# An encoder layer on one core: large tiles on multiples of 512 bytes, and another way into the first and out of the last matmul

## The chip, the cores and the metric

One core of a Trainium2 chip runs the whole program. The metric is the device time of one execution in microseconds (us), the median of three runs. A core has five engines that work side by side: TensorE (PE, matmuls, with its weight loads shown apart as PEld), VectorE (DVE), ScalarE (ACT), GpSimd (POOL) and SyncE (SP, which here only issues DMAs). They read and write the on-chip memory (SBUF, 128 partitions), TensorE writes its results to eight PSUM banks of 128 x 512 floats.

## The reference

One encoder layer over 256 tokens of 2048 features, in float32: a SwiGLU feed-forward block (FFN) with half weight, a mixer (a Hyena convolution group beside a differential-attention group), and a second FFN, with a layer norm behind each.

```python
x = layer_norm(ALPHA * x + 0.5 * swiglu(x, ffn1_w_gate, ffn1_w_up, ffn1_w_down), ln1_g, ln1_b)
y = hybrid_mixer(x, w_in, ..., w_out, lam_init)
x = layer_norm(ALPHA * x + y, ln2_g, ln2_b)
x = layer_norm(ALPHA * x + 0.5 * swiglu(x, ffn2_w_gate, ffn2_w_up, ffn2_w_down), ln3_g, ln3_b)

def swiglu(x, w_gate, w_up, w_down):
    return (jax.nn.silu(x @ w_gate) * (x @ w_up)) @ w_down      # D_FF = 5632
def layer_norm(x, g, b):
    mu = jnp.mean(x, -1, keepdims=True); var = jnp.mean(jnp.square(x - mu), -1, keepdims=True)
    return (x - mu) * lax.rsqrt(var + 1e-5) * g + b
```

## The kernel before

**Arithmetic.** Every float32 operand of a matmul is split into a rounded high part (`hi`, made by ACT as a cast) and the rest (`lo`, made by DVE as a subtraction). A product is hi x hi + hi x lo + lo x hi: three matmuls (`mm3`), or two where the stream side holds `[hi | lo]` side by side (`xx[:, k]`, 512 columns), as in the gate and up projections (`ws_block`: L368 with 512 columns, L369 with 256).

**Weights.** All weights pass through a list of units of 512 KB. `fetch` issues the DMA of a unit on SP into one of four `raw` buffers, `prepare` issues its cast and subtraction (L171, L172), `nextunit` hands it to the matmuls. A unit of a gate or up matrix holds 4 k-tiles of 256 columns, one of a down matrix 2 k-tiles of 512 columns. `halves` cuts the DMA and the split of the first two units into two.

**Order.** The kernel is written in program order; small side jobs are put between units (`beside`, `tick`). Instructions of one engine then run in the order in which the scheduler of the language has laid them down; `after(a, b)` holds a behind b on its engine.

**Head.** The transposed input `x_t` comes in eight pieces of 2 k-tiles (256 KB, tiles `xt0`), all on SP, with the first weight units between them. `xt_chunk("0", c, ...)` casts and subtracts them into `xx`. Twelve matmuls on a tile of ones (`warm(12)`, each shown as two rows, L296) keep TensorE busy until then.

**Down projection and layer norm.** `as_chunk` makes the output in four chunks of 512 columns (c = 0 to 3), for two groups of tokens (j = 0, 1). For the last `lead` units of chunk 3 `as_block` does all of j = 0 before j = 1, so that the sums of j = 0 are read while TensorE still works on j = 1. `add_rows` adds a chunk to the residual `res` (L323) and takes its statistics (L324); `ln_stats` makes mean and 1/sigma (L328, L330, a power on POOL at L331). `last_rows` does this for chunk 3. Between layers `normalise` and `xt_chunk` follow: subtract the mean and scale, transpose on TensorE, apply g and b, split.

**Tail.** After the last FFN `finish(j, c, on_pool)` writes the result: for chunks 0 to 2 two DVE operations, (res - mean) x g (L1024) and x 1/sigma + b (L1025); for chunk 3 one ACT operation and two POOL operations (L1020 to L1022). Each chunk leaves by a DMA of 256 KB from SP (L1026).

**Memory.** SBUF is given out in the order of the pools: `const` (`res` 16 KB per partition, `xx` 32 KB, `ident`, `ones`, `mhalf` of 8 bytes, two `pvt`, `stats` of 192 bytes), then the weight buffers, then the small tiles, then the FFN's `hh` and `hl`. In the built program `res` and `xx` begin 128 bytes behind a multiple of 512, the weight and `xt0` buffers 352 bytes behind one (32 behind a multiple of 64), `hh` and `hl` 416 behind one.

Of the kernel before, what the change touches and what calls it, by code (L numbers as in the profile page):

```python
# [17 lines left out]
P = 128  # L18
# [56 lines left out]
def kernel(ctx: ExitStack, tc: tile.TileContext, a: dict, out: bass.AP):  # L75
# [69 lines left out]
    def halves(i, k):  # L145

        return [slice(0, k // 2), slice(k // 2, k)] if i < 2 else [slice(0, k)]

# [9 lines left out]
    def prepare(n):  # L158
        while st["split"] < min(n, len(units)):
            i = st["split"]  # L160
            _, k, c, name = units[i]
            late = i - (len(units) - LEAD)
            if 0 <= late < 4:

                hi, lo = (xx[:, 4 * late + 2 * q:4 * late + 2 * q + 2].rearrange("p k a l -> p k (a l)") for q in range(2))
            else:
                hi = wp.tile([P, k, c], F32R, tag="whi", name=f"hi{name}")
                lo = wp.tile([P, k, c], F32R, tag="wlo", name=f"lo{name}")
            raw = raws.pop(i)
            for s_ in halves(i, k):  # L170
                i1 = nc.scalar.copy(out=hi[:, s_], in_=raw[:, s_])  # L171
                i2 = nc.vector.tensor_tensor(out=lo[:, s_], in0=raw[:, s_], in1=hi[:, s_].bitcast(F32), op=ALU.subtract)  # L172
# [55 lines left out]
    nc.gpsimd.memset(ones, 1.0)
    mhalf = const.tile([P, 2], F32, name="mhalf")
    nc.gpsimd.memset(mhalf, -0.5)  # L230
# [31 lines left out]
    hy_g = [pvt[1][:, NV + i:NV + i + 1] for i in range(8)]  # L262

    def xt_chunk(tag, c, g, b):
        for kp in (2 * c, 2 * c + 1):
            hs = xx[:, 2 * kp:2 * kp + 2, 0, :]
            ls = xx[:, 2 * kp:2 * kp + 2, 1, :]
            if g is None:
                i1 = nc.scalar.copy(out=hs, in_=xt0[kp])
# [48 lines left out]

    stats = const.tile([P, 2, 4, 6], F32, name="stats")

    def add_rows(ps, j, c, scale):
        cs = slice(c * 512, (c + 1) * 512)
        nc.vector.scalar_tensor_tensor(out=res[:, j, cs], in0=ps, scalar=scale, in1=res[:, j, cs], op0=ALU.mult, op1=ALU.add)  # L323
        nc.vector.bn_stats(out=stats[:, j, c, :], in_=res[:, j, cs])  # L324

    def ln_stats(tag, j):
        mv = sm.tile([P, 2], F32, tag="mv", name=f"mv{tag}{j}")
        nc.vector.bn_aggr(out=mv, in_=stats[:, j, :, :])  # L328
        rs = sm.tile([P, 1], F32, tag="rs", name=f"rs{tag}{j}")
# [44 lines left out]

    def as_block(pd, lhs, use, n_k):

        for j in range(2):
            for k0, (h, lo) in use:
                for k in range(2):
                    kk = k0 + k  # L380
                    xh_, xl_ = lhs(kk, j)
                    mm3(pd[j], xh_, xl_, h[:, k, :], lo[:, k, :], kk == 0, kk == n_k - 1)

    def as_chunk(pd, lhs, n_k, lead=1):
# [4 lines left out]
        use = [(ku * 2, nextunit()) for ku in range(n - lead, n)]  # L389
        as_block(pd, lhs, use, n_k)  # L390


    def ffn(tag, first, down_side=None, gate_side=None, filler=None, lead=2):
        with tc.tile_pool(name=f"ffn{tag}", bufs=1, reuse_waits="tile") as fp:
# [616 lines left out]

    ln = ffn("3", first2, last_vectors(), lead=LEAD)
    ov = out[0].rearrange("(p j) d -> p j d", j=2)

    def finish(j, c, on_pool):
        cs = slice(c * 512, (c + 1) * 512)
        r, gt, bt = res[:, j, cs], gb3["ln3_g", c], gb3["ln3_b", c]
        mean, rs, nm = ln[j]
        if on_pool:
            nc.scalar.activation(out=r, in_=r, func=AF.Identity, bias=nm, scale=rs)  # L1020
            nc.gpsimd.tensor_tensor(out=r, in0=r, in1=gt, op=ALU.mult)  # L1021
            nc.gpsimd.tensor_tensor(out=r, in0=r, in1=bt, op=ALU.add)  # L1022
        else:
            nc.vector.scalar_tensor_tensor(out=r, in0=r, scalar=mean, in1=gt, op0=ALU.subtract, op1=ALU.mult)  # L1024
            nc.vector.scalar_tensor_tensor(out=r, in0=r, scalar=rs, in1=bt, op0=ALU.mult, op1=ALU.add)  # L1025
        nc.sync.dma_start(out=ov[:, j, cs], in_=r)  # L1026

    for j in range(2):
        nc.vector.scalar_tensor_tensor(out=ln[j][2], in0=ln[j][0], scalar=-1.0, in1=ln[j][1], op0=ALU.mult, op1=ALU.mult)
# [30 lines left out]
```

## Time and profile before

| what | value |
|---|---|
| median of 3 runs | 1960.94 us (1959.08 to 1961.29) |
| the profiled execution | 1963.29 us, of which 1961.2 us are the span that the profile shows |
| TensorE busy in the span | 1932.8 us (99%), 10,260 matmul rows |
| DVE, ACT, POOL busy | 62%, 47%, 16% |
| DMA | 376.43 MB, 192 GB/s on average, 57.6% of 16 DMA engines on SP's queue |
| first matmul on data / end of the last one | 8.05 us / 1946.95 us after the span's start |
| mean granted TensorE clock | 0.995 |

How to read it: times are counted from the span's start. A timeline row has start, duration, engine, line, operation, output<-inputs, shape, and in brackets how long the engine was idle before and what released it. Durations of matmuls overlap; the distance between two starts is what one costs. A row of windows has the stretch, its length, the busy time of PE, PEld, DVE, ACT and POOL with their instruction counts, the granted clock (1.00 is full speed), the DMA share and GB/s. The 1963.29 us of the profiled execution are the span and 2.1 us around it, and 2.35 us above the median.

### The profile page before, as it was taken

The numbers are of one execution on the slowest core, as the hardware profiler recorded it, in microseconds if no ns is written. First come the engines' busy times: TensorE is split into PE (matmuls) and PEld (weight loads), VectorE is DVE, ScalarE is ACT, GpSimd is POOL, SyncE is SP. The second block draws the span as 40 slices with busy tenths as digits, with TensorE's granted clock in tenths as the row PEclk, the third lists the DMA queues.
The fourth block names the chain that finished last, engine by engine and source line by source line (L and its number), as shares of the span: only waits on it lengthen the run. The fifth ranks groups of instructions, "written<-read, shape, count | busy, mean of one in ns | idle before, by whom it ended". The sixth has DMA issues, their size and how long they took to land. (4 is left out here: it accounts for less than half of the span.)

```text
span 1961.2 us, 27062 instructions
## 1 busy us (share of the span) xinstructions
PE 1932.8 (99%) x10260; PEld 1656.4 (84%) x10260; DVE 1215.4 (62%) x1538; ACT 926.1 (47%) x1334; POOL 305.3 (16%) x330
## 2 busy tenths in 40 slices
PE   9999999999999999999999999999999999999997
PEld 8888888888888887888887878888888888888885
DVE  5555556555566656899978666755555555544445
ACT  5554444544444435545555534545444544433332
POOL 4221111121100002012222011312111121100001
PEclk9999999999999999999999999999999999999999
DMA  8656656656666656655575444865656556555553
GB/s 288 204 187 192 190 189 198 192 185 193 203 208 214 204 191 207 220 181 153 172 226 161 158 154 157 274 191 187 192 191 193 187 189 194 187 189 187 189 186 115
DMA packets 294698, 376.43 MB, mean 192 GB/s; under 512 B 13263, under 2 KB 222312, under 8 KB 294568
## 3 DMA queue, kind: packets, MB, share of 16 engines
q1 hardware_dynamic: 289832, 361.90, 57.6%
q0 software_dynamic: 4736, 12.82, 2.2%
q8 instruction: 80, 1.31, 0.3%
q14 instruction: 50, 0.41, 0.1%
HBM read 366.27 MB, written 8.39 MB: 191 GB/s over the span
## 5 line engine op out<-in xcount | busy, mean ns | idle before, releaser
L368 PE MATMUL ps<-xx,hi1g 128*128 128x512 f32 x1408 | 490.2, 391 | 1.5 <-ACT hi1g L171 1.5
L368 PE MATMUL ps<-xx,hi2g 128*128 128x512 f32 x1408 | 488.6, 390 | 1.1 <-DVE xx L95 1.1
L369 PE MATMUL ps<-xx,lo1g 128*128 128x256 f32 x1408 | 397.4, 283 | 0.1
L369 PE MATMUL ps<-xx,lo2g 128*128 128x256 f32 x1408 | 397.0, 282 | 0.0
L172 DVE TENSOR_TENSOR lo2g<-raw2g,hi2g 128x1024 fp32r<-128x1024 f32 x176 | 234.8, 1335 | 179.6 <-ACT hi2g L171 179.6
L172 DVE TENSOR_TENSOR lo1g<-raw1g,hi1g 128x1024 fp32r<-128x1024 f32 (+1 forms) x178 | 232.5, 1308 | 177.6 <-ACT hi1g L171 177.6
L368 PEld LDWEIGHTS ps<-xx,hi1g 128*128 128x128 f32 x1408 | 264.8, 188 | 58.2 <-ACT hi1g L171 1.7
L368 PEld LDWEIGHTS ps<-xx,hi2g 128*128 128x128 f32 x1408 | 264.3, 188 | 56.4 <-ACT xt L282 1.3
L171 ACT CAST hi2g<-raw2g 128x1024 fp32r<-128x1024 f32 x176 | 185.0, 1052 | 187.3 <-PE ps L368 174.9
L171 ACT CAST hi1g<-raw1g 128x1024 fp32r<-128x1024 f32 (+1 forms) x178 | 185.2, 1042 | 179.7 <-PE ps L368 170.7
L369 PEld LDWEIGHTS ps<-xx,lo1g 128*128 128x128 f32 x1408 | 266.7, 190 | 0.7 <-DVE lo1g L172 0.5
L369 PEld LDWEIGHTS ps<-xx,lo2g 128*128 128x128 f32 x1408 | 266.1, 189 | 0.1
L404 POOL TENSOR_TENSOR hf<-hf,sg 128x256 f32<-128x256 f32 x88 | 64.7, 755 | 741.8 <-DVE hf L373 741.7
L172 DVE TENSOR_TENSOR lo2d<-raw2d,hi2d 128x1024 fp32r<-128x1024 f32 x84 | 103.6, 1233 | 118.7 <-ACT hi2d L171 118.7
L171 ACT CAST hi1d<-raw1d 128x1024 fp32r<-128x1024 f32 x88 | 92.4, 1050 | 132.0 <-PE pd L92 119.7
L171 ACT CAST hi2d<-raw2d 128x1024 fp32r<-128x1024 f32 x84 | 88.4, 1052 | 138.7 <-PE pd L92 131.0
L172 DVE TENSOR_TENSOR lo1d<-raw1d,hi1d 128x1024 fp32r<-128x1024 f32 x88 | 107.2, 1221 | 72.7 <-ACT hi1d L171 72.7
L90 PE MATMUL pd<-hi1d,hh 128*128 128x512 f32 x352 | 139.3, 396 | 0.0
L368 PE MATMUL ph<-xx,hihy 128*128 128x512 f32 x384 | 137.0, 397 | 2.2 <-DVE xx L95 1.1
L92 PE MATMUL pd<-hi1d,hl 128*128 128x512 f32 x352 | 139.1, 395 | 0.0
L91 PE MATMUL pd<-lo1d,hh 128*128 128x512 f32 x352 | 139.1, 395 | 0.0
L90 PE MATMUL pd<-hi2d,hh 128*128 128x512 f32 x336 | 132.9, 395 | 0.0
(380 smaller groups left out, 3078.8 us busy)
## 6 DMA issues: line engine op xcount, KB each, us to landing
raw1d<-in_ffn_w_down_dram SPq DMA_DIRECT2D x88, 512.0 KB, 4.3
raw2g<-in_ffn_w_gate_dram SPq DMA_DIRECT2D x88, 512.0 KB, 3.5
raw2g<-in_ffn_w_up_dram SPq DMA_DIRECT2D x88, 512.0 KB, 3.5
raw2d<-in_ffn_w_down_dram SPq DMA_DIRECT2D x88, 512.0 KB, 4.2
raw1g<-in_ffn_w_gate_dram SPq DMA_DIRECT2D x87, 512.0 KB, 3.5
raw1g<-in_ffn_w_up_dram SPq DMA_DIRECT2D x87, 512.0 KB, 3.9
rawhy<-in_w_in_dram SPq DMA_DIRECT2D x48, 512.0 KB, 4.5
rawat<-in_w_in_dram SPq DMA_DIRECT2D x48, 512.0 KB, 4.2
```

Of the source, the lines that this page charges most:

```text
L90: mm(out=o, lhsT=lh, rhs=rh, start=start, stop=False)
L91: mm(out=o, lhsT=lh, rhs=rl, start=False, stop=False)
L92: mm(out=o, lhsT=ll, rhs=rh, start=False, stop=stop)
L171: i1 = nc.scalar.copy(out=hi[:, s_], in_=raw[:, s_])
L172: i2 = nc.vector.tensor_tensor(out=lo[:, s_], in0=raw[:, s_], in1=hi[:, s_].bitcast(F32), op=ALU.subtract)
L368: mm(out=ps[t], lhsT=h[:, k, ts_], rhs=xx[:, kk].rearrange("p a l -> p (a l)"), start=kk == 0, stop=False)
L369: mm(out=ps[t][:, :L], lhsT=lo[:, k, ts_], rhs=xx[:, kk, 0, :], start=False, stop=kk == KD - 1)
L404: nc.gpsimd.tensor_tensor(out=hf, in0=hf, in1=sg, op=ALU.mult)
```

## The change

Four edits come together.

1. **Places in SBUF.** The small constants move ahead of `res` and `xx`, two unused spaces are put in (`line`), `nlam` and `g08` leave the mixer's pool, the filter's three weights share one `t512` buffer. In the built program `res`, `xx`, all weight buffers, the `t512` buffers, `hh`, `hl` and the mixer's large tiles then begin at a multiple of 512 bytes.
2. **Head.** The first two pieces of `x_t` are issued from ACT's queue, the first as two DMAs of one k-tile; unit 0 comes in four pieces; the second piece of x is cast behind the first two quarters of unit 0 (`xt_first`).
3. **Last chunk of the FFNs and of the output projection.** For j = 1 chunk 3 is two halves of 256 columns in two PSUM banks (`last_banks`). In the last `lead` units the first half is done whole before the second (`apart`).
4. **Tail.** ACT and POOL no longer take part in chunk 3. For j = 1 the multiplication with g of chunks 2 and 3 is done ahead of the statistics where it can be (`times_g`); b - mean/sigma x g for these 1024 columns is made by TensorE as a product of a 2 x 128 tile (rows: -mean/sigma, and ones) with a 2 x 256 tile (rows: g and b), four times (`pb`); DVE then does x 1/sigma + that, in pieces of 512, 256 and 256 columns.

```diff
+    def line(pool, n):
+        pool.tile([P, n // 4], F32, name="space", tag="space", bufs=1)
     def halves(i, k):
-        return [slice(0, k // 2), slice(k // 2, k)] if i < 2 else [slice(0, k)]
+        n = (4, 2)[i] if i < 2 else 1
+        return [slice(q * k // n, (q + 1) * k // n) for q in range(n)]
...
+                if i == 0 and s_.stop == 2:
+                    xt_first(1, i1, i2)
...
+    mhalf = const.tile([P, 2], F32, name="mhalf")
+    stats = const.tile([P, 2, 5, 6], F32, name="stats")
+    line(const, 384 - 32 - 256)
+    ident = const.tile([P, P], F32, name="ident")
...
-        nc.sync.dma_start(out=xt0[kp], in_=a["x_t"][:, 2 * kp:2 * kp + 2, :])
+        if kp == 0:
+            for i in range(2):
+                nc.scalar.dma_start(out=xt0[kp][:, i], in_=a["x_t"][:, i, :])
+        else:
+            (nc.scalar if kp == 1 else nc.sync).dma_start(out=xt0[kp], in_=a["x_t"][:, 2 * kp:2 * kp + 2, :])
...
+    def xt_first(kp, a1=None, a2=None):
+        hs = xx[:, 2 * kp:2 * kp + 2, 0, :]
+        ls = xx[:, 2 * kp:2 * kp + 2, 1, :]
+        for k_ in ([slice(0, 1), slice(1, 2)] if kp == 0 else [slice(0, 2)]):
+            i1 = nc.scalar.copy(out=hs[:, k_], in_=xt0[kp][:, k_])
+            i2 = sub(nc.vector, ls[:, k_], xt0[kp][:, k_], hs[:, k_])
...
-    def last_rows(tag, pd, scale):
+    def last_rows(tag, pd, scale, between=None):
         ln = []
-        for j in range(2):
-            add_rows(pd[j], j, 3, scale)
-            ln.append(ln_stats(tag, j))
+        add_rows(pd[0], 0, 3, scale)
+        ln.append(ln_stats(tag, 0))
+        for half in range(2):
+            add_rows(pd[1][half], 1, 3, scale, half)
+            if between is not None and half == 0:
+                between()
+        ln.append(ln_stats(tag, 1))
...
+        go(pd[0], 0, slice(0, 512), ks)
+        if not isinstance(pd[1], list):
+            go(pd[1], 1, slice(0, 512), ks)
+            return
+        for ks_ in ([ks] if apart else [[k] for k in ks]):
+            for half in range(2):
+                go(pd[1][half][:, :256], 1, slice(half * 256, (half + 1) * 256), ks_)
...
+    def ln_rows():
+        nc.gpsimd.memset(lh2, 1.0)
+        for q in range(4):
+            t = sm.tile([P, L], F32, tag="sg" if q < 2 else "hf", name=f"gb2_{q}")[:2]
+            for r, nme in enumerate(("ln3_g", "ln3_b")):
+                nc.gpsimd.dma_start(out=t[r:r + 1, :], in_=a[nme][0:1, 1024 + q * L:1024 + (q + 1) * L])
...
+    def early_g():
+        times_g(1, 2)
+        times_g(1, 3, 0)
...
-    for j in range(2):
-        nc.vector.scalar_tensor_tensor(out=ln[j][2], in0=ln[j][0], scalar=-1.0, in1=ln[j][1], op0=ALU.mult, op1=ALU.mult)
-        for c in range(4):
-            finish(j, c, c == 3)
+    for c in range(4):
+        centre(0, c)
+        scale_add(0, slice(c * 512, (c + 1) * 512), gb3["ln3_b", c])
+    mean, rs, nm = ln[1]
+    centre(1, 0)
+    after(times_g(1, 3, 1), last["rs"])
+    nc.vector.scalar_tensor_tensor(out=nm, in0=mean, scalar=-1.0, in1=rs, op0=ALU.mult, op1=ALU.mult)
+    pn = bank("pn")
+    mm(out=pn[:1, :P], lhsT=nm, rhs=ident, start=True, stop=True)
+    nc.scalar.copy(out=lh2[:1, :], in_=pn[:1, :P])
+    pb = [bank(f"pb3_{i}") for i in range(2)]
+    for q in range(4):
+        mm(out=pb[q // 2][:, q % 2 * L:(q % 2 + 1) * L], lhsT=lh2, rhs=gb2[q], start=True, stop=True)
+    scale_add(1, slice(0, 512), gb3["ln3_b", 0])
+    centre(1, 1)
+    scale_add(1, slice(512, 1024), gb3["ln3_b", 1])
+    scale_add(1, slice(1024, 1536), pb[0])
+    for q in range(2):
+        scale_add(1, slice(1536 + q * L, 1536 + (q + 1) * L), pb[1][:, q * L:(q + 1) * L])
```

How the order moves, at three places. ACT at the start of the program before (`xt_0`, `xt_1` are the pieces of x, `raw1g_0_0` is unit 0 and `raw1g_0_1` unit 1; the last column is partitions x elements):

```order
L269 ACT_TABLE_LOAD
L269 CAST xx<-xt_0_71 128x2x256
L269 CAST xx<-xt_1_76 128x2x256
L171 CAST hi1g_0_0_140<-raw1g_0_0_73 128x512 x2
L269 CAST xx<-xt_2_78 128x2x256
L171 CAST hi1g_0_1_146<-raw1g_0_1_80 128x512 x2
```

And ACT at the start now:

```order
L238 DMA xt_0_78<-in_x_t_dram 128x256 x2
L240 DMA xt_1_86<-in_x_t_dram 128x512
L285 ACT_TABLE_LOAD
L285 CAST xx<-xt_0_78 128x256 x2
L176 CAST hi1g_0_0_145<-raw1g_0_0_81 128x256 x2
L285 CAST xx<-xt_1_86 128x2x256
L176 CAST hi1g_0_0_145<-raw1g_0_0_81 128x256 x2
L176 CAST hi1g_0_1_157<-raw1g_0_1_90 128x512 x2
L285 CAST xx<-xt_2_88 128x2x256
```

Half of unit 0 no longer stands behind the second piece of x, and unit 1 no longer behind the third; three DMA issues stand ahead of the table load.

DVE behind the last matmul before (`pd_3_1` is chunk 3 of j = 1):

```order
L323 SCALAR_TENSOR_TENSOR res<-pd_3_1_16759,res 128x512
L324 BN_STATS stats<-res 128x6
L328 BN_AGGR mv_17144<-stats 128x2
L330 TENSOR_SCALAR rs_17146<-mv_17144 128x1
L1024 SCALAR_TENSOR_TENSOR res<-res,mv_17144,ln_g_15548 128x512
L1029 SCALAR_TENSOR_TENSOR nm_17149<-mv_17144,rs_17146 128x1
L1024 SCALAR_TENSOR_TENSOR res<-res,mv_17144,ln_g_15588 128x512
L1025 SCALAR_TENSOR_TENSOR res<-res,rs_17146,ln_b_15550 128x512
L1025 SCALAR_TENSOR_TENSOR res<-res,rs_17146,ln_b_15590 128x512
L1024 SCALAR_TENSOR_TENSOR res<-res,mv_17144,ln_g_15628 128x512
L1025 SCALAR_TENSOR_TENSOR res<-res,rs_17146,ln_b_15630 128x512
```

And DVE behind the last matmul now (`pd_3_11` is the second half of it, `pb` what TensorE makes of g and b):

```order
L346 SCALAR_TENSOR_TENSOR res<-pd_3_11_16968,res 128x256
L347 BN_STATS stats<-res 128x6
L351 BN_AGGR mv_17489<-stats 128x2
L353 TENSOR_SCALAR rs_17491<-mv_17489 128x1
L1086 SCALAR_TENSOR_TENSOR res<-res,mv_17489,ln_g_15743 128x512
L1069 TENSOR_TENSOR res<-res,ln_g_15863 128x256
L1099 SCALAR_TENSOR_TENSOR nm_17494<-mv_17489,rs_17491 128x1
L1090 SCALAR_TENSOR_TENSOR res<-res,rs_17491,ln_b_15745 128x512
L1086 SCALAR_TENSOR_TENSOR res<-res,mv_17489,ln_g_15783 128x512
L1090 SCALAR_TENSOR_TENSOR res<-res,rs_17491,ln_b_15785 128x512
L1090 SCALAR_TENSOR_TENSOR res<-res,rs_17491,pb_0_17514 128x512
L1090 SCALAR_TENSOR_TENSOR res<-res,rs_17491,pb_1_17515 128x256 x2
```

The first two operations are half as wide, and chunk 3 is written by DVE at the end, behind TensorE's `pb`.

TensorE's end now, its last data matmuls and what follows them:

```order
L94 MATMUL pd_3_11_16968<-hi2d_21_17327,hh_11210 128x256
L95 MATMUL pd_3_11_16968<-lo2d_21_17328,hh_11210 128x256
L96 MATMUL pd_3_11_16968<-hi2d_21_17327,hl_11211 128x256
L1101 MATMUL pn<-ident,nm_17494 1x128
L1105 MATMUL pb_0_17514<-gb_0_15922,pvt_74 128x256
L1105 MATMUL pb_0_17514<-gb_1_15925,pvt_74 128x256
L1105 MATMUL pb_1_17515<-gb_2_15928,pvt_74 128x256
L1105 MATMUL pb_1_17515<-gb_3_15931,pvt_74 128x256
```

Before, the program's last matmul was one of 512 columns into `pd_3_1`, and nothing stood behind it; five matmuls that wait for `nm` are new.

More of the change, by code (lines that the diff above doesn't have):

```diff
@@ L212, in finish_side @@
             tick()
+    mhalf = const.tile([P, 2], F32, name="mhalf")
+    stats = const.tile([P, 2, 5, 6], F32, name="stats")
+    line(const, 384 - 32 - 256)
+    ident = const.tile([P, P], F32, name="ident")
+    ones = const.tile([P, P], F32, name="ones")
+    pvt = [const.tile([P, P], F32, name="pvt0"), const.tile([P, P], F32, name="pvt1")]
     res = const.tile([P, 2, D], F32, name="res")
@@ L220 @@
         xt0.append(t512(f"xt0_{kp}", (2, L)))
-        nc.sync.dma_start(out=xt0[kp], in_=a["x_t"][:, 2 * kp:2 * kp + 2, :])
+        if kp == 0:
[3 more added lines that the diff above has]
+            (nc.scalar if kp == 1 else nc.sync).dma_start(out=xt0[kp], in_=a["x_t"][:, 2 * kp:2 * kp + 2, :])
         if kp % 2 == 0:
             fetch(kp // 2 + 1)
-    ident = const.tile([P, P], F32, name="ident")
+    line(sm, 384)
     make_identity(nc, ident)
-    ones = const.tile([P, P], F32, name="ones")
     nc.gpsimd.memset(ones, 1.0)
-    mhalf = const.tile([P, 2], F32, name="mhalf")
     nc.gpsimd.memset(mhalf, -0.5)
@@ L262 @@
     hy_g = [pvt[1][:, NV + i:NV + i + 1] for i in range(8)]
+    def xt_first(kp, a1=None, a2=None):
[4 more added lines that the diff above has]
+            i2 = sub(nc.vector, ls[:, k_], xt0[kp][:, k_], hs[:, k_])
+        if kp == 0:
+            hold["act"], hold["dve"] = i1, i2
+        elif a1 is not None:
+            after(i1, a1)
+            after(i2, a2)
     def xt_chunk(tag, c, g, b):
@@ L317, in scale_residual, with add_rows @@
                 yield 1
[L319 to L322 removed]
+    def add_rows(ps, j, c, scale, half=None):
+        cs = slice(c * 512, (c + 1) * 512) if half is None else slice(c * 512 + half * 256, c * 512 + (half + 1) * 256)
+        ps = ps if half is None else ps[:, :256]
         nc.vector.scalar_tensor_tensor(out=res[:, j, cs], in0=ps, scalar=scale, in1=res[:, j, cs], op0=ALU.mult, op1=ALU.add)
[L324 removed]
+        nc.vector.bn_stats(out=stats[:, j, c + (half or 0), :], in_=res[:, j, cs])
     def ln_stats(tag, j):
         mv = sm.tile([P, 2], F32, tag="mv", name=f"mv{tag}{j}")
[L328 removed]
+        nc.vector.bn_aggr(out=mv, in_=stats[:, j, :4 + j, :])
         rs = sm.tile([P, 1], F32, tag="rs", name=f"rs{tag}{j}")
@@ L425, in ffn @@
             for c in range(4):
-                pd = [bank(f"pd{tag}_{c}_{j}") for j in range(2)]
+                pd = [bank(f"pd{tag}_{c}_{j}") for j in range(2)] if c < 3 else last_banks(f"pd{tag}_{c}")
                 as_chunk(pd, lhs, KF, lead if c == 3 else 1)
@@ L981 @@
     for c in (2, 3):
-        pd = [bank(f"pwo{c}_{j}") for j in range(2)]
+        pd = [bank(f"pwo{c}_{j}") for j in range(2)] if c == 2 else last_banks(f"pwo{c}")
         as_chunk(pd, wo_lhs, KD, c - 1)
@@ L1010, in last_vectors, with times_g @@
             yield 2
-    ln = ffn("3", first2, last_vectors(), lead=LEAD)
+    lh2 = pvt[0][:2, :]
+    gb2 = []
+    def ln_rows():
[4 more added lines that the diff above has]
+                nc.gpsimd.dma_start(out=t[r:r + 1, :], in_=a[nme][0:1, 1024 + q * L:1024 + (q + 1) * L])
+            gb2.append(t)
+    def times_g(j, c, half=None):
+        cs = slice(c * 512, (c + 1) * 512) if half is None else slice(c * 512 + half * 256, c * 512 + (half + 1) * 256)
+        gs = slice(0, 512) if half is None else slice(half * 256, (half + 1) * 256)
+        return nc.vector.tensor_tensor(out=res[:, j, cs], in0=res[:, j, cs], in1=gb3["ln3_g", c][:, gs], op=ALU.mult)
@@ L1013, with last_side, centre @@
+    def early_g():
+        times_g(1, 2)
+        times_g(1, 3, 0)
+    def last_side():
+        yield from last_vectors()
+        yield 1
+        ln_rows()
+    ln = ffn("3", first2, last_side(), lead=LEAD, between=early_g)
     ov = out[0].rearrange("(p j) d -> p j d", j=2)
-    def finish(j, c, on_pool):
+    def centre(j, c):
         cs = slice(c * 512, (c + 1) * 512)
[L1017 to L1025, printed above, removed]
-        nc.sync.dma_start(out=ov[:, j, cs], in_=r)
@@ L1028, with scale_add @@
-    for j in range(2):
-        nc.vector.scalar_tensor_tensor(out=ln[j][2], in0=ln[j][0], scalar=-1.0, in1=ln[j][1], op0=ALU.mult, op1=ALU.mult)
-        for c in range(4):
-            finish(j, c, c == 3)
+        r = res[:, j, cs]
+        nc.vector.scalar_tensor_tensor(out=r, in0=r, scalar=ln[j][0], in1=gb3["ln3_g", c], op0=ALU.subtract, op1=ALU.mult)
+    def scale_add(j, cs, b):
+        r = res[:, j, cs]
+        nc.vector.scalar_tensor_tensor(out=r, in0=r, scalar=ln[j][1], in1=b, op0=ALU.mult, op1=ALU.add)
+        nc.sync.dma_start(out=ov[:, j, cs], in_=r)
```

42 lines of the change are left out of this document (20 added, 22 removed).

## The prediction

> **What bounds the kernel now.** I read the engine table first, then windows over the whole span, then the timelines of the head, of the layer-norm boundaries and of the tail.
>
> ```profile
> PE 1932.8 (99%) x10260; PEld 1656.4 (84%) x10260; DVE 1215.4 (62%) x1538; ACT 926.1 (47%) x1334; POOL 305.3 (16%) x330
> ...
> 50.00:500.00 450.00, 450.00 (x2590) 397.44 (x2589) 254.70 (x270) 220.13 (x329) 81.24 (x83) 1.00 0.61 192
> 1900.00:1947.00 47.00, 46.95 (x202) 37.48 (x200) 25.09 (x26) 14.85 (x15) 4.17 (x3) 1.00 0.43 145
> 1947.00:1962.00 15.00, 0.00 (x0) 0.00 (x0) 8.02 (x11) 0.81 (x1) 4.10 (x3) 0.66 0.19 70
> ```
>
> TensorE has no gap in the long stretches; DVE, ACT and the DMAs have room there. So a faster side engine or DMA is worth nothing between about 20 us and the end of the last matmul, except at the two layer norms. Three things can move the time: when TensorE starts and how fast it runs at first, how much it has to do, and the 14.2 us behind its last matmul (1946.95 to 1961.2), where it has nothing to do.
>
> **The head.**
>
> ```profile
> 1.12 5.42 PE L296 MATMUL ps_warm<-ones 128*128 128x128 f32 x24 [1.12 <-POOL ones L228]
> 4.04 0.62 ACT L269 CAST xx<-xt 128x512 fp32r<-128x512 f32 x1 [2.04 <-DMA xt<-in_x_t_dram]
> 6.86 0.62 ACT L269 CAST xx<-xt 128x512 fp32r<-128x512 f32 x1 [2.19 <-DMA xt<-in_x_t_dram]
> 7.38 1.14 ACT L171 CAST hi1g<-raw1g 128x512 fp32r<-128x512 f32 x2
> 8.05 0.74 PE L368 MATMUL ps<-xx,hi1g 128*128 128x512 f32 x2 [1.50 <-ACT hi1g L171]
> 13.01 1.05 ACT L171 CAST hi1g<-raw1g 128x1024 fp32r<-128x1024 f32 x1 [0.87 <-DMA raw1g<-in_ffn_w_gate_dram]
> 14.09 1.23 DVE L172 TENSOR_TENSOR lo1g<-raw1g,hi1g 128x1024 fp32r<-128x1024 f32 x1 [1.22 <-ACT hi1g L171]
> 16.09 0.40 PE L369 MATMUL ps<-xx,lo1g 128*128 128x256 f32 x2
> ...
> 9.00:10.00 1.00, 1.00 (x7) 0.92 (x8) 1.00 (x3) 0.72 (x3) 0.39 (x2) 0.88 1.05 383
> 10.00:11.00 1.00, 1.00 (x4) 0.87 (x4) 1.00 (x3) 0.91 (x2) 0.50 (x2) 0.50 1.08 363
> ...
> 13.00:14.00 1.00, 1.00 (x7) 0.92 (x6) 0.00 (x0) 0.99 (x2) 0.53 (x2) 0.91 1.10 345
> ```
>
> The first cast of unit 0 (7.38) stands behind the cast of the second piece of x, which waits for its DMA until 6.86. In the new order it waits only for the first k-tile and a quarter of unit 0, which should be there by about 4 to 5 us. But TensorE is busy with its ones until 6.54, so its start moves from 8.05 to about 6.5: 1.5 us. The 1.5 us gap before 8.05 is also followed by a stretch at half clock (0.88 and then 0.50 from late in 9 to 10 us, full again early in 13 to 14). Without the gap it may go too: about 3.4 us at half speed, 1.7 us of work. That is the upper end, 3.2 us.
>
> It is not reached, because the data set the pace soon after. Unit 2 lands at 13.01 with the DMAs already full (share 1.08, 363 GB/s), its `lo` is ready at 14.09 + 1.23 = 15.32, and TensorE uses it at 16.09. However early TensorE starts, it can't pass this point more than 0.8 us sooner unless unit 2 lands sooner, and the bytes ahead of unit 2 are the same as before: a second queue changes who issues them, not how many. Lower end: with idle gaps again, another half-clock stretch comes while TensorE should catch up, a loss of 1.7 us. I take a gain of 0.8, the row nearest to the limit. The three DMA issues that now stand ahead of ACT's table load cost nothing as long as the first piece lands after them; that cover is 4.04 us long.
>
> **More matmuls.** Chunk 3 of j = 1 is cut in two. That replaces 44 + 16 + 44 = 104 k-tiles x 3 = 312 matmuls of 512 columns by 624 of 256, each with its own weight load. Prices, as distances between starts:
>
> ```profile
> 1929.77 0.40 PE L92 MATMUL pd<-xx,hl 128*128 128x512 f32 x1
> 1930.00 0.40 PE L90 MATMUL pd<-hi2d,hh 128*128 128x512 f32 x1
> 1930.24 0.39 PE L91 MATMUL pd<-lo2d,hh 128*128 128x512 f32 x1
> ...
> 764.20 0.28 PE L92 MATMUL pik<-xx 128*128 128x256 f32 x1
> 764.32 0.28 PE L90 MATMUL pik<-xx 128*128 128x256 f32 x1
> ```
>
> 0.233 us for 512 columns, 0.12 for 256 (the filter's products, where each has its own weight load as here). So 312 x (0.240 - 0.233) = +2 us, on the path. I take +1.9, with 0.1195 for 0.12.
>
> **The two layer-norm boundaries.**
>
> ```profile
> 763.45 0.69 DVE L323 SCALAR_TENSOR_TENSOR res<-pd,res 128x512 f32<-128x512 f32 x1 [0.89 <-PE pd L92]
> 764.05 0.14 DVE L851 TENSOR_SCALAR g<-pvt 128x1 f32<-128x1 f32 x1
> 764.17 0.69 DVE L324 BATCH_NORM_STATS2 stats<-res 128x6 f32<-128x512 f32 x1
> ...
> 768.43 0.43 DVE L95 TENSOR_TENSOR xx<-xt,xx 128x256 fp32r<-128x256 f32 x1
> 769.94 0.69 DVE L95 TENSOR_TENSOR xx<-xt,xx 128x512 fp32r<-128x512 f32 x1
> ```
>
> Behind the last matmul of a layer DVE adds and takes statistics, and TensorE waits for it. Half the width saves 0.26 us (0.69 against 0.43) in each of the two: 0.5 us at each boundary. At the first, the stray L851 moves away (it is laid early now): 0.1 more. Together -1.1. Next in line are the power on POOL and the transposes, unchanged.
>
> **The tail.**
>
> ```profile
> 1937.78 1.01 POOL L331 TENSOR_TENSOR rs<-rs,mhalf 128x1 f32<-128x1 f32 x1 [232.73 <-DVE rs L330]
> ...
> 1946.98 0.69 DVE L323 SCALAR_TENSOR_TENSOR res<-pd,res 128x512 f32<-128x512 f32 x1 [2.48 <-PE pd L92]
> 1947.71 0.69 DVE L324 BATCH_NORM_STATS2 stats<-res 128x6 f32<-128x512 f32 x1
> 1949.99 0.16 DVE L1029 SCALAR_TENSOR_TENSOR nm<-mv,rs 128x1 f32<-128x1 f32 x1 [0.44 <-POOL rs L331]
> 1950.73 2.41 DVE L1025 SCALAR_TENSOR_TENSOR res<-res,rs,ln_b 128x512 f32<-128x512 f32 x2
> 1952.67 1.59 POOL L1022 TENSOR_TENSOR res<-res,ln_b 128x512 f32<-128x512 f32 x1
> 1953.07 1.74 DVE L1024 SCALAR_TENSOR_TENSOR res<-res,mv,ln_g 128x512 f32<-128x512 f32 x1
> 1954.85 0.75 DVE L1025 SCALAR_TENSOR_TENSOR res<-res,rs,ln_b 128x512 f32<-128x512 f32 x1
> ...
> L1056 POOLq DRAIN  x3: 46/98/7762, 1952.6 to 1960.9; - x3
> L1056 SPq DRAIN  x3: 7/7/7, 1958.0 to 1960.7; - x3
> 1051.23 0.59 PE L781 MATMUL pbat<-dgat,ones 128*128 128x256 f32 x2
> ```
>
> Count from T, the end of the last matmul (1946.95). Before, DVE ends at T+8.65. Two of its operations take 1.74 and 2.41 / 2 us instead of 0.75, in the very time in which POOL works. Now: add 0.47, statistics 0.47, L1086 and the half multiplication with g in the shadow of the power (1.0), `nm` at T+2.5 (before T+3.0), then four operations of 0.7 and two of 0.45, with POOL silent: the end at T+6.3, 2.3 us earlier. The eight small loads of g and b on POOL are free (POOL stood idle for 232.73 us ahead of L331), `times_g` of chunk 2 falls where DVE is busy 25 of 47 us.
>
> What is late next is `pb`. `nm` is ready at T+2.7; a product of 256 float32 columns takes two passes, 0.59 - 0.38 = 0.21 us apart, so 0.43 at full clock, 0.86 at half. With the transposition and ACT's copy the four products end at about T+5.4 at full clock (in time) or T+7.2 at half, and then DVE ends at T+7.8, only 0.85 earlier. TensorE idles from T to T+2.7, longer than the 1.5 us after which the clock halved in the head, so half clock in part is the likelier: 1.6.
>
> By the Trainium skill ("TensorE: Matmul & The Clock Gate", Part 1) the clock halves only after at least one idle window of about 3.4 us; by that, `pb` runs at full clock and the gain is the whole 2.3. The trace differs: 1.5 us were enough in the head.
>
> Then comes the end of the program. SP is through at 1958.0, 2.4 us behind DVE; but the last long row is POOL's drain, from 1952.6 for 7.76 us, to 1960.4, and the span ends 0.8 later. POOL's last work ends at 1954.26. If this drain takes its 6.1 us from POOL's last work, it now ends at T+2.5+6.1, ahead of SP, and 2.3 us more go. If it hangs on SP's end, nothing more. One row can't tell; I take half, 1.1. Tail: -2.7, between -0.85 and -4.6.
>
> **The sum.** -0.8 + 1.9 - 1.1 - 2.7 = -2.7 us. Against the profiled execution of 1963.29 that is 1960.6; it lies 2.35 above the median, so the median of the runs comes to 1960.94 - 2.7 = 1958.2. With all ends added it is -7.0 to +1.7.
>
> **The places in SBUF.** I cost them at nothing in the sum. In the rows at 1929.77 to 1930.24 the stream comes first from `xx` (128 behind a multiple of 512) and then from `hi2d` (352 behind, so 32 behind a multiple of 64), and the distance to the next is 0.23 and 0.24: if starts off a 64-byte boundary cost anything, these would differ. DVE's 0.69 for 512 and 0.43 for 256 elements are alike for both kinds of tile. Only a step at 512 itself would not show, since no large tile starts there now.
>
> **Rivals.**
>
> *The array reads faster from the new places.* For it speaks that something besides the clock slows matmuls:
>
> ```profile
> 10.63 0.63 PE L368 MATMUL ps<-xx,hi1g 128*128 128x512 f32 x1
> 11.28 0.63 PE L368 MATMUL ps<-xx,hi1g 128*128 128x512 f32 x1
> ...
> 100.11 0.39 PE L368 MATMUL ps<-xx,hi1g 128*128 128x512 f32 x1
> 100.46 0.39 PE L368 MATMUL ps<-xx,hi1g 128*128 128x512 f32 x1
> ```
>
> A pair (512 and 256 columns) costs 0.64 at half clock and 0.35 at full, where half of 0.64 would be 0.32. If places are part of these 28 ns, each ns per pair is worth 5 us (10,260 / 2 pairs). Against it speak the equal rows above. A tenth to a fifth of the excess, 3 to 6 ns, gives 1928 to 1943; it decides from 0.3 ns.
> The Trainium skill ("SBUF — State Buffer", Specifications) puts SBUF's lines at 16 bytes; all tiles start on one already, so by it this rival gives nothing. No run here shows that yet.
>
> *The halves are bound by their weight loads* (slower). A load is 84% of the time busy as it is; twice as many for the same columns. If a 256-column matmul took 0.15 instead of 0.12, that is 624 x 0.03 = +18.7 us and 1977; it decides from 0.13 (+6). Against it: the filter's rows at 0.12, with a load each.
>
> *The ends are hidden.* Unit 2 lands as late as before, `pb` runs at half clock, POOL's drain hangs on SP: 0 + 1.9 - 1.1 - 0.85 = 0, so 1961.
>
> **How the numbers follow.** A measurement of this kernel can tell about 0.2% from no change, 3.9 us. Chances: the forecast 0.55, faster reads 0.24, hidden ends 0.13, loads 0.08. The forecast's own range is 1954 to 1961; a third of it passes 1957.0. Faster: 0.19 + 0.23, so 0.42; slower: 0.08 and a little of the hidden ends, 0.09; the rest, 0.49, within 0.2%. The range reaches from 1947, which leaves out some half of the fast reads, to 1963, which leaves out the loads.
>
> **What would show it.** First data matmul at 6.5 us, unit 2's cast still near 13; matmuls into the halves 0.12 apart; L346 of 256 elements at 0.43 to 0.48; DVE's last operation at T+6.3 to T+7.8 without any of 1.7 us; the place of POOL's drain against SP's. Wrong would be above all a steady distance other than 0.233 or a pair other than 0.35.

## The result, and the profile after

The changed kernel takes 1946.44 us (median of four runs, 1943.8 to 1950.55), the one before 1961.12 in the same rounds: ratio 0.9928, 95% interval 0.9909 to 0.9947, so 14.7 us faster. Five more rounds, later, gave 1945.03 against 1963.34, ratio 0.9908 (0.9894 to 0.9922). Forecast were 1958.2, 2.7 us faster, with a low end of 1947.

The two profiled executions lie further apart than the medians: 1963.29 before (2.2 above its median), 1943.8 after (2.6 below). Their spans differ by 19.2 us, and this is how these fall to the stages, worked out from the starts in the two traces. The gate and up stages run from their first matmul to the next stage's, the loops behind them (down projections, hyena, attention, output projection) from their first matmul to their last, a boundary from there to the next stage; the 2.0 us behind the hyena loop and the 2.0 us behind attention's, alike in both, have no row.

| stage | before | after | change |
|---|---|---|---|
| to the first matmul on data | 8.05 | 6.28 | -1.8 |
| gate and up products of the first FFN | 492.8 | 494.7 | +1.9 |
| down projection, first FFN | 262.2 | 258.0 | -4.2 |
| two layer-norm boundaries | 6.0 + 6.0 | 5.4 + 5.4 | -1.2 |
| hyena products | 166.9 | 164.4 | -2.5 |
| attention's input products | 161.8 | 160.0 | -1.7 |
| output projection | 101.9 | 101.0 | -0.9 |
| gate and up products of the second FFN | 490.8 | 490.8 | 0 |
| down projection, second FFN | 246.1 | 241.3 | -4.8 |
| behind the start of the last matmul | 14.6 | 10.7 | -3.9 |

More than half lies in the down projections, attention and the output projection, long loops of 512-column products. TensorE was busy all the time in the windows of such loops below, and is so now. Windows inside the first down projection, the second gate and up stage and the second down projection (columns: stretch, its length, PE busy with the count of matmuls, weight loads, DVE, ACT, POOL, granted clock, DMA share, GB/s); first before, then after:

```profile
550.00:650.00 100.00, 100.00 (x470) 82.48 (x469) 65.50 (x85) 43.13 (x53) 6.42 (x12) 1.00 0.66 209
1300.00:1400.00 100.00, 100.00 (x579) 88.67 (x578) 55.77 (x56) 49.03 (x74) 19.07 (x20) 1.00 0.60 190
1760.00:1860.00 100.00, 100.00 (x430) 80.57 (x429) 48.71 (x44) 37.28 (x36) 0.00 (x0) 1.00 0.57 189
```

```profile
550.00:650.00 100.00, 100.00 (x485) 84.56 (x484) 66.72 (x87) 44.64 (x55) 6.41 (x12) 1.00 0.68 220
1300.00:1400.00 100.00, 100.00 (x579) 87.43 (x578) 54.12 (x53) 47.92 (x71) 15.29 (x16) 1.00 0.61 190
1760.00:1860.00 100.00, 100.00 (x443) 82.83 (x442) 46.98 (x42) 39.03 (x37) 0.00 (x0) 1.00 0.61 194
```

Read the counts. At the same full clock, with PE busy 100% in both, the second down projection does 443 matmuls in 100 us instead of 430: 226 ns for one instead of 233. The gate and up stage does 579 in both. So the loops of three 512-column products (hi x hi, lo x hi, hi x lo) became faster, the pairs of 512 and 256 columns (gate and up) did not. The busy share says nothing of it; the count in a window does.

The head after: rows of the timeline (those between are left out), then two windows:

```profile
6.28 1.11 PE L395 MATMUL ps<-xx,hi1g 128*128 128x512 f32 x2
...
11.83 1.05 ACT L176 CAST hi1g<-raw1g 128x1024 fp32r<-128x1024 f32 x1 [0.57 <-DMA raw1g<-in_ffn_w_gate_dram]
12.91 1.23 DVE L177 TENSOR_TENSOR lo1g<-raw1g,hi1g 128x1024 fp32r<-128x1024 f32 x1 [0.68 <-ACT hi1g L176]
12.93 0.74 PE L395 MATMUL ps<-xx,hi1g 128*128 128x512 f32 x2 [0.30 <-ACT hi1g L176]
14.19 0.50 PE L396 MATMUL ps<-xx,lo1g 128*128 128x256 f32 x2 [0.53 <-DVE lo1g L177]
...
16.19 1.05 ACT L176 CAST hi1g<-raw1g 128x1024 fp32r<-128x1024 f32 x1 [2.28 <-DMA raw1g<-in_ffn_w_up_dram]
```

```profile
12.00:13.00 1.00, 0.70 (x5) 0.38 (x3) 0.32 (x2) 1.00 (x2) 0.00 (x0) 1.00 0.96 305
13.00:14.00 1.00, 0.66 (x2) 0.22 (x2) 1.00 (x1) 0.92 (x2) 0.00 (x0) 1.00 0.91 305
```

TensorE starts 1.8 us sooner and never falls to half clock, but waits at unit 2 (busy 0.70 and 0.66) and again at unit 3, whose cast begins at 16.19 behind 2.28 us of waiting for its DMA (16.13 before). At the first down projection both kernels are level: 500.81 before, 500.97 after.

The first add at a boundary and the tail after, in the timeline; then a window of `pb`, and the drains by their line. T, the end of the last matmul on data, is about 1931.62:

```profile
759.33 0.42 DVE L346 SCALAR_TENSOR_TENSOR res<-pd,res 128x256 f32<-128x256 f32 x1 [0.50 <-PE pd L96]
...
1931.66 0.42 DVE L346 SCALAR_TENSOR_TENSOR res<-pd,res 128x256 f32<-128x256 f32 x1 [3.18 <-PE pd L96]
...
1933.14 0.99 POOL L354 TENSOR_TENSOR rs<-rs,mhalf 128x1 f32<-128x1 f32 x1 [10.00 <-DVE rs L353]
1934.16 0.16 DVE L1099 SCALAR_TENSOR_TENSOR nm<-mv,rs 128x1 f32<-128x1 f32 x1
...
1935.10 3.24 PE L1105 MATMUL pb<-gb,pvt 2*128 2x256 f32 x8 [0.34 <-ACT pvt L1102]
...
1936.67 0.75 DVE L1090 SCALAR_TENSOR_TENSOR res<-res,rs,pb 128x512 f32<-128x512 f32 x1 [0.24 <-PE pb L1105]
1938.38 0.87 DVE L1090 SCALAR_TENSOR_TENSOR res<-res,rs,pb 128x256 f32<-128x256 f32 x2 [0.96 <-PE pb L1105]
```

```profile
1936.00:1937.00 1.00, 1.00 (x4) 0.81 (x3) 0.76 (x2) 0.00 (x0) 0.00 (x0) 0.50 0.54 209
```

```profile
L1136 POOLq DRAIN  x3: 46/102/7815, 1933.1 to 1941.8; - x3
L1136 SPq DRAIN  x3: 7/7/7, 1941.2 to 1941.5; - x3
```

`nm` comes at T+2.5, as forecast; `pb` runs at half clock (0.50 in the window from 1936) and DVE waits for it twice (0.24, 0.96), so DVE ends at 1938.38 + 0.87 = T+7.6. POOL's drain again lasts 7.8 us, and again it starts where the row of POOL's last operation starts: 1952.6 before, beside the addition at 1952.67, and 1933.1 now, beside the power at 1933.14. It ends at 1940.9 and no longer sets the end. SP does, at 1941.2, only 0.3 us later; in `e1_ends_only` below the drain still came last, at 1953.7 against 1953.3.

### The profile page after: what moved, and what is told of

Same layout as the page of the kernel before. It is cut to its first block, busy times and chain, and to the rows that moved or that the text cites. A ratio compares the mean times of both kernels' runs of the same rounds, so it can differ in the third digit from the quotient of the medians.

```text
span 1942.0 us, 27741 instructions
## 1 busy us (share of the span) xinstructions
PE 1922.5 (99%) x10582; PEld 1659.8 (85%) x10582; DVE 1214.3 (63%) x1552; ACT 925.7 (48%) x1336; POOL 302.9 (16%) x335
## 5 line engine op out<-in xcount | busy, mean ns | idle before, releaser
L396 PE MATMUL ps<-xx,lo1g 128*128 128x256 f32 x1408 | 391.5, 279 | 1.1 <-DVE lo1g L177 1.1
L396 PE MATMUL ps<-xx,lo2g 128*128 128x256 f32 x1408 | 390.0, 277 | 0.0
L95 PE MATMUL pd<-lo1d,hh 128*128 128x512 f32 (+1 forms) x396 | 145.2, 367 | 0.0
L94 PE MATMUL pd<-hi1d,hh 128*128 128x512 f32 (+1 forms) x396 | 145.1, 366 | 0.0
L96 PE MATMUL pd<-hi1d,hl 128*128 128x512 f32 (+1 forms) x396 | 144.8, 366 | 0.0
L95 PE MATMUL pd<-lo2d,hh 128*128 128x512 f32 (+1 forms) x372 | 137.3, 369 | 0.0
```

Source lines behind the costliest of these rows:

```text
L94: mm(out=o, lhsT=lh, rhs=rh, start=start, stop=False)
L95: mm(out=o, lhsT=lh, rhs=rl, start=False, stop=False)
L96: mm(out=o, lhsT=ll, rhs=rh, start=False, stop=stop)
L396: mm(out=ps[t][:, :L], lhsT=lo[:, k, ts_], rhs=xx[:, kk, 0, :], start=False, stop=kk == KD - 1)
```

## The experiments

**Both halves of the change alone.** `e1_ends_only`: the placing hunks taken back, with spaces that put every large tile where it was before; head, halves and tail stay (cut to the main lines, comments added).

```diff
-    stats = const.tile([P, 2, 5, 6], F32, name="stats")      # and ident, ones, pvt ahead of res
-    line(const, 384 - 32 - 256)
...
-    line(sm, 384)
...
+    line(const, 192)          # weights at 352, hh and hl at 416, as before
```

> The changed kernel with every large tile where it stood before (res and xx 128 behind a multiple of 512, weights 352, hidden layer 416, mixer 416 and 480); head, halves and tail as changed. If the places gave the gain in the loops of 512-column products: their distance goes back from 226-227 to 231-235 ns, and the time is 1961.1 less what the ends give in the two traces (head 0.2, boundaries 1.2, tail 3.9, halves +2) = 1957 to 1959. If the ends and the missing stretches at half clock gave it: 1945 to 1948, as the changed kernel.

`e2_places_only`: the reverse, the placing hunks alone in the kernel before.

> The kernel before with only the places changed (everything large at multiples of 512); head, boundaries, halves and tail as before. If the places gave the gain: 512-column products of the down projections 226-227 ns apart, last matmul 11 to 13 us earlier, tail still 14 us, 1948 to 1950. If the ends gave it: 231-235 ns and 1960 to 1962.

| | median us | ratio to before (95%) | down projections | attention | behind the last matmul's start |
|---|---|---|---|---|---|
| `e1_ends_only` | 1957.09 | 0.9978 (0.9969 to 0.9987) | 261.5, 246.4 | 161.8 | 10.4 |
| `e2_places_only` | 1949.79 | 0.9935 (0.9920 to 0.9950) | 255.8, 239.2 | 160.0 | 14.6 |

Against 1961.23 for the kernel before the ends alone give 4.1 us, the places alone 11.4; together 15.5, beside the 14.7 and 18.3 of the whole in its two measurements. The places are the larger part, and the theory that head, tail and clock gave the whole gain has fallen. Window 1760 to 1860 of `e1_ends_only`, then of `e2_places_only`:

```profile
1760.00:1860.00 100.00, 100.00 (x430) 80.60 (x429) 47.68 (x43) 37.36 (x36) 0.00 (x0) 1.00 0.60 189
```

```profile
1760.00:1860.00 100.00, 100.00 (x443) 82.81 (x442) 46.99 (x41) 39.04 (x37) 0.00 (x0) 1.00 0.62 195
```

**Which operand.** In the down projections the weights are streamed and the hidden layer is loaded. `e4_w352` puts only hi and lo back, `e5_h416` only hh and hl.

```diff
+                if i == 0:
+                    wp.tile([P, 88], F32, name="gap1", tag="gap1", bufs=1)      # e4: hi, lo 352 further
                 hi = wp.tile([P, k, c], F32R, tag="whi", name=f"hi{name}")
...
-    line(sm, 384)
+    line(sm, 32)                                                                # e4: so that all else stays
...
+            fp.tile([P, 104], F32, name="gap1", tag="gap1", bufs=1)             # e5: hh, hl 416 further
             hh = fp.tile([P, KF, L], F32R, name=f"hh{tag}")
```

> The changed kernel with only the split weights (hi, lo) put back to 352 behind a multiple of 512; they are the streamed operand in the down projections and the loaded one in the gate and up products. If the start of the streamed operand matters: down projections 231-235 ns for 512 columns, 5 us longer each (time + 11 to 13). If the loaded operand matters there: 226-227 as in the changed kernel. In the gate and up stage the pair (512 and 256 columns) should stay at 346-348 by either.

> The changed kernel with only the hidden layer (hh, hl) put back to 416 behind a multiple of 512; it is the loaded operand of the down projections and the written one in the gate and up stage. If the start of the loaded operand matters: down projections back at 231-235 ns, time + 10. If the streamed one matters: 226-227 ns, and the time of the changed kernel.

1962.52 and 1955.83 us. From here on most kernels have one run, and the changed kernel's own runs lie up to 6.75 us apart; so the readings go by the stages of the traces, not by the total times. Down projections: 263.3 and 247.0, 263.2 and 247.2. Their windows, `e4_w352` first:

```profile
1760.00:1860.00 100.00, 100.00 (x431) 80.42 (x430) 48.65 (x44) 37.30 (x36) 0.00 (x0) 1.00 0.60 189
```

```profile
1760.00:1860.00 100.00, 100.00 (x430) 80.45 (x429) 46.44 (x41) 37.59 (x36) 0.00 (x0) 1.00 0.59 188
```

Both theories of a single guilty operand miss: either one moved alone costs the whole 6 ns for each product, and both moved (before) cost no more.

**Where the step lies.** `e6_h64_h128` and `e7_h256_h32` shift hh and hl by one amount in the first FFN and by another in the second, with the same gap as in `e5`.

> The changed kernel with the hidden layer 64 behind a multiple of 512 in the first feed-forward and 128 behind in the second. If the step is at 512 (or 256): both down projections at 231-237 ns for 512 columns, + 5 us each. If it is at 128: only the first. If it is at 64: neither, and the time of the changed kernel.

> The changed kernel with the hidden layer 256 behind a multiple of 512 in the first feed-forward and 32 behind in the second. If the step is at 512: both slow (231-237 ns). If it is at 256, 128 or 64: the first stays at 226-227, the second is slow. If nothing but 416 itself does it: neither.

1955.36 and 1954.97 us. Windows of `e6_h64_h128`, then of `e7_h256_h32`:

```profile
550.00:650.00 100.00, 100.00 (x470) 82.40 (x469) 64.79 (x85) 43.65 (x53) 6.42 (x12) 1.00 0.67 211
1760.00:1860.00 100.00, 100.00 (x432) 81.08 (x431) 46.76 (x41) 37.78 (x36) 0.00 (x0) 1.00 0.58 188
```

```profile
550.00:650.00 100.00, 100.00 (x480) 84.31 (x479) 68.55 (x90) 44.74 (x55) 6.41 (x12) 1.00 0.68 217
1760.00:1860.00 100.00, 100.00 (x430) 80.55 (x430) 46.31 (x41) 37.84 (x36) 0.00 (x0) 1.00 0.58 186
```

64, 128 and 32 are slow, 256 is not (480 where the changed kernel has 485 and before 470; its down projection takes 258.0, as in the changed kernel). The step is at 256, not 512.

**Multiples or distance.** `w256` puts hi and lo at 256 (the gap of `e4` with 64 floats), `s_all128` everything large at 128:

```diff
-    line(const, 384 - 32 - 256)
+    line(const, 384 - 32 - 256 + 128)
```

> The changed kernel with the split weights (hi and lo) 256 behind a multiple of 512. If the step is at 256 for the streamed operand too, as it was for the loaded one: down projections 226-228 ns for 512 columns, 258 and 241 us, the gate pair 347, time of the changed kernel (1944 to 1951). If the stream needs 512: 231-237 and 5 us more in each.

> The changed kernel with every large tile 128 further, so all at 128 behind a multiple of 512. If each operand's own place counts: down projections 231-236 ns, attention 161.7, time of the kernel with the ends only (1955 to 1959). If the distance between the streamed and the loaded operand counts: 226-228 and the time of the changed kernel.

1943.82 and 1946.48 us; down projections 258.1 and 241.3 in both, attention 160.2 and 160.0. `s_all128`:

```profile
1760.00:1860.00 100.00, 100.00 (x443) 82.86 (x442) 46.98 (x42) 39.03 (x37) 0.00 (x0) 1.00 0.65 194
```

With every tile 128 off, nothing is lost. So it isn't the multiples that count but the distance between the start of the streamed and that of the loaded operand, modulo 256. Before, for example, the weights stream from 352 and the hidden layer is loaded from 416: -64, which is 192 modulo 256. The layouts so far, sorted by the distance (mean distance between the starts of two 512-column products, over 900 to 1,050 of them in each down projection):

| streamed minus loaded, modulo 256 | kernels | ns per product |
|---|---|---|
| 0 | after, `e2`, `w256`, `s_all128`, `e7` first FFN | 226.7 to 227.8 |
| 96 | `e4`, `e5` | 233.2 to 233.4 |
| 128 | `e6` second FFN | 232.5 |
| 192 | before, `e1`, `e6` first FFN | 233.1 to 233.3 |
| 224 | `e7` second FFN | 233.2 |

The Trainium skill ("TensorE: Matmul & The Clock Gate", Part 2) calls the read ports of the streamed and the loaded operand independent. In these runs they aren't so in their effect: the place of one against the other decides what a product costs, 6 ns. Whether it is the ports that do this isn't shown, and distances of 64 and 160 for all three products weren't measured.

**Attention, and the gate pair.** `e3_xx128` moves xx alone by 128; `x1` and `x2` move it by another amount in each of three stages.

```diff
+    xxs = const.tile([P, KD * 2 * L + 64], F32R, name="xx")
+    def xx_at(off):
+        return xxs[:, off // 4:off // 4 + KD * 2 * L].rearrange("p (k a l) -> p k a l", a=2, l=L)
+    xx = xx_at(64)       # 32 from the mixer on, 192 in the second FFN; x2: 96, 224, 160
```

> The changed kernel with only xx put back to 128 behind a multiple of 512. xx is streamed in the gate, up and hyena products and loaded in the attention's. If either operand off its place is enough (as the hidden layer and the weights each were, alone): attention's 512-column products back from 227 to 231-235 ns, that stage + 1.7 us, the down projections unchanged at 226-227, time + 2. If a distance of 128 is harmless and only starts off a multiple of 64 cost (before, 352 and 416 were): no change anywhere.

> The changed kernel with xx 64 behind a multiple of 256 in the first feed-forward, 32 in the mixer, 192 in the second feed-forward; all else at multiples of 256. If the distance between the streamed and the loaded operand counts (modulo 256): attention, which loads xx, back at 161.5 to 162 us (distance -32), the down projections unchanged at 258 and 241. In the gate and up pair, 832 cycles of 2.4 GHz (346.7 ns, 32 for each product beside its columns) is what nearly every layout gave so far; if that is a floor, the pair is 347 or, as with xx at 128, 353. If a distance exists at which the 256-column product costs 113 and the 512-column one stays at 227: 340, and 10 us less in that stage.

> The same with xx at 96, 224 and 160 behind a multiple of 256 in the three places. By the distance: attention 161.5 to 162, down projections unchanged; pair 347 to 353, where 96 gives 347 (weights at 352 and xx at 0 were 160 apart and gave 347). If there is a better distance: 340 and 10 us less in that stage.

1959.54, 1964.68 and 1955.67 us. Attention goes back to 161.6, 162.1 and 161.9, the down projections stay at 258.0 to 258.4 and 241.3 to 241.4: the distance again, with 128, 224 and 32 in attention. That `e3` cost over 10 us and not 2 was foreseen by neither theory: the gate pair got slower, and the two gate and up stages took 6.1 and 6.3 us longer than in the changed kernel. Second gate and up stage of `e3_xx128`, then of `x1`:

```profile
1300.00:1400.00 100.00, 100.00 (x571) 87.64 (x570) 54.71 (x55) 48.68 (x73) 19.10 (x20) 1.00 0.60 187
```

```profile
1300.00:1400.00 100.00, 100.00 (x569) 86.83 (x568) 54.56 (x55) 49.45 (x76) 19.14 (x20) 1.00 0.61 185
```

By distance (now `xx` minus weights) the pair takes, as the mean distance from one pair's start to the next one's: 0, 347 ns; 32 (before), 347; 64, 353; 96, 350; 128, 351; 160, 347; 192, 353. So the pair does go by the distance, but the old layout happened to stand at one of its good ones: 128 - 352 is 32 modulo 256. There was nothing to gain there. No distance gave less than 347 on average, the sum of 226.7 and 120.

**One low half moved.** `e8_lo352` and `x3_lo64` shift only lo, by 352 and 64.

> The changed kernel with only the low halves of the split weights at 352 behind a multiple of 512. If a product is slow by its own operands: of the three products of a k-tile only the one that streams lo goes to 231-237 ns, the two others stay at 226-227, + 1.7 us for each down projection. If a slow start spoils the neighbours' weight loads too: two of three are slow. In the gate and up stage lo is the loaded operand of the 256-column product: that one goes from 116 to 113-118.

> The changed kernel with only the low halves of the weights 64 behind a multiple of 512. In the gate and up pair the 512-column product loads hi at distance 0, the 256-column one lo at -64, the distance at which 256-column products took 113 ns in the run with the hidden layer at 64. If each product goes by its own two operands: 227 + 113 = 340, 10 us less in each gate and up stage, and + 1.7 us in each down projection, 1928 to 1935. If the pair is bound to its sum: 347 or more, and the time 4 to 10 us above the changed kernel.

1955.3 and 1955.27 us. Down projections 261.1 and 244.7, 261.8 and 245.5: with one product of three off its place, about six to seven tenths of what `e4` and `e5` lose. In `e8` the product of lo takes 233.8 in the first FFN, the one before it, of hi, 231.5, and the third 228.6; in the second FFN it is 230.9, 233.2 and 229.2, so there the neighbour pays more than the product of lo. A product isn't priced by its own two operands alone. The gate pair stayed at 347, so no 340.

**Without the halves.** `v1_no_halves` keeps chunk 3 whole everywhere, `v2_halves_last` cuts it in the second FFN only.

```diff
-                pd = [bank(f"pd{tag}_{c}_{j}") for j in range(2)] if c < 3 else last_banks(f"pd{tag}_{c}")
+                pd = [bank(f"pd{tag}_{c}_{j}") for j in range(2)]
```

> The changed kernel with the last 256 columns no longer apart: all of chunk 3 in products of 512 columns, in both feed-forwards and in the output projection; places, head and the rest of the tail as changed. If the halves now cost more than they bring (with the new places 512 columns take 226.7 ns and two halves 240, so 13 ns for each of 312): down projections and output projection 2.2 + 0.9 + 2.1 us shorter, boundaries 0.6 longer each, tail 0.8 longer, together -3.2: 1943. If the halves pay at the ends as the change means it: 1947 or more.

> The same, but the halves kept in the second feed-forward alone, in front of the tail. If the halves cost everywhere: 2.2 + 0.9 - 1.2 = 1.9 us less than the changed kernel, and 1.3 more than without any: 1944.5. If they pay in the tail: less than without any, 1942.

> The changed kernel itself, once more in five rounds, so that its ratio stands on more runs beside those without the halves (0.9908 and 0.9919). By the stages of the traces it is 1.3 us slower than without any halves: 1945 to 1946, ratio 0.992. If the halves pay: 0.990 or less.

1943.86 (ratio 0.9908, 0.9894 to 0.9921), 1943.88 (0.9919, 0.9904 to 0.9933), and the changed kernel again 1945.03 (0.9908, 0.9894 to 0.9922). By the stages `v1` is 1.9 + 0.9 + 2.1 us shorter in the three projections, 1.2 longer at the boundaries and 1.7 behind the last matmul, 2.0 better in all; the times can't tell the three apart. No version beats the changed kernel by what can be measured.

## Why the prediction was wrong, step by step

- **The places in SBUF: the step that failed.** They were costed at nothing and gave 11.4 us alone. The argument was that a stream from `xx` (128) and one from `hi2d` (352) cost the same 0.23 to 0.24, so starts don't matter. The runs show in its place that a product costs by the distance of its two operands, 226.7 to 227.8 ns at 0 and 232.5 to 233.4 at 96, 128, 192 and 224 (before: 192). The two rows were no contrast: against `hl` and `hh` at 416 the distances are 224 and 192, both slow. Two equal rows only exclude an effect that would have to differ between them. The prediction named the gap in this ("no large tile starts there now") and left it at a rival with a chance of 0.24. The sign that it gave for being wrong, a steady distance other than 0.233, is what came.
- **The rival "array reads faster"** had the cause and the direction. It priced pairs, 5 us per ns in 5,130 of them; in truth 6 ns are saved in some 3,070 products of the three-product loops and none in 2,816 gate pairs and 384 of the hyena part. In places-only against before: 6.4 + 7.0 + 1.8 + 1.7 = 16.9 us, of which 5.6 were lost in that execution in the first gate and up stage (below). The rule on 16-byte lines ("SBUF — State Buffer", Specifications, in the Trainium skill), by which this rival gives nothing, doesn't cover it: all starts here are multiples of 16, and 227 and 233 ns stand beside each other.
- **More matmuls, +1.9.** With the old places the halves were free (`e1` against before: -0.8, +0.1 and +0.3 us in the three projections; halves 113 to 118 ns apart). With the new ones they take 120 as priced, but the whole 512 takes 226.7 and no longer 233, so they cost 1.9 + 0.9 + 2.1 = 4.9 us (`v1`). The two parts of the change work against each other, and the sum took them one by one.
- **Head, -0.8: nothing came of it.** First matmul 6.28 instead of 6.5, no half clock, and still level at 500.9. Unit 2 set the pace as said, but it wasn't the last to do so: unit 3, whose cast begins at 16.19 (before 16.13), took the rest, and behind it the lead was 0.2 us.
- **Boundaries, -1.1:** -1.2, right.
- **Tail, -2.7:** -3.9 (-3.2 to -4.3 in the other traces with the new tail and the halves). The DVE chain ended at T+7.6, near the bound for half clock, so its part was 1.0 and not 1.6; POOL's drain hung on POOL's last operation and not on SP, so its term came whole, 2.3 and not 1.1. The Trainium skill's rule on the clock ("TensorE: Matmul & The Clock Gate", Part 1), full clock unless an idle window of about 3.4 us has passed, differs from the trace again: 2.8 us without a matmul, and 0.50 from 1936 on.
- **Not in the sum: hyena, -2.5.** Before has two stretches at half clock there (two of the rows below), the profiled run after has none.

```profile
878.00:880.00 2.00, 2.00 (x9) 1.81 (x9) 2.00 (x7) 0.00 (x0) 0.00 (x0) 0.50 0.86 248
922.00:924.00 2.00, 2.00 (x10) 1.81 (x9) 2.00 (x2) 0.04 (x1) 1.92 (x1) 0.50 0.35 136
```

`e4` has two as well, `e1`, `e2`, `e3`, `e6`, `x1`, `x2` and `x3` have one, `e5`, `e7`, `e8` and the six traces with all distances at 0 and the new head none. They seem to come and go in one kernel too: executions of the kernel before had a mean granted clock from 0.998 (1959.34 us) to 0.993 (1964.34). What makes them come isn't shown, and the length of the wait ahead of them doesn't decide it: 1.5 us without a matmul stand ahead of the second one in the kernel before (918.35 to 919.86), while 2.6 us in the same stage of the changed kernel (869.22 to 871.78) bring none. So the -2.5 isn't shown to come from the change.

The ends as a whole came out near, -2.7 forecast and -4.1 measured alone, in part by luck: with the old places the halves cost nothing instead of 1.9, the head gave nothing instead of 0.8, and the tail gave 4.3 in that trace instead of 2.7.

**Left open.** Why a distance costs what it does inside the chip; why 256-column products are cheaper (113 to 118) at some of the distances where 512-column ones are dearer, so that the pair's sum hardly moves; and why pairs took some 353 ns on average instead of 347 for the first 300 us in some executions (`e2`: 568 matmuls between 100 and 200 us instead of 579, `e7`: 569). Such a loss, 5.6 us in `e2`, may be what lets the changed kernel's runs lie 6.75 us apart, and why the profiled pair differs more than the medians; no trace was taken of the slower of these runs.

## What to carry to other kernels

Where TensorE is busy all the time, count the matmuls in a window of each long loop and compare with columns over clock: the rest per product (here 13 to 20 ns) is a cost of its own, and the place of the operands can be part of it. Try the streamed and the loaded operand of long float32 product loops at the same place modulo 256 bytes, as paid here, and measure each loop, for a layout that suits one can be bad for the next. To say that a property costs nothing, compare with a row where it is absent, not two rows that both have it.

## What the runs showed of the hardware

- A product of 512 columns, of float32 split in two parts and with its own weight load, cost 226.7 ns on average at best (`e2`, second FFN) and 233 with the wrong distance; one of 256 columns cost 120 and 113 to 118. At 2.4 GHz (an estimate from 120 and 226.7: 256 columns more for 106.7 ns) that is 32 cycles beside the columns, against 48 and some 16 to 27. The Trainium skill ("TensorE: Matmul & The Clock Gate", Part 2) gives 216 ns for 512 back to back; no loop here came below 226 on average.
- Moving one tile by 128 bytes (`e3`) cost some 13 us in 1946, in one run; the two gate and up stages alone took 12.4 us longer in its trace. All the places together had gained 11.4.
- POOL's drain at the end takes 7.8 us from the start of POOL's last operation, before and after (7,762 and 7,815 ns), though that was an addition of 1.59 us in the one and a power of 0.99 us in the other; ending POOL's part early hides it, here by 0.3 us.
